# A 4096 x 4096 matrix product with bias and tanh: B's first block in one transfer per column half, visits by column halves, and the last products in another order

## The chip, the cores and the metric

The kernel runs on one core of a Trainium2 chip. The metric is the device time of one execution in microseconds. Below, PE or TensorE is the matrix engine, DVE or VectorE the vector engine, ACT or ScalarE the engine for activations and copies, POOL or GpSimd the engine that here only issues transfers (it casts B and A to fp16 on the way), and SP or SyncE the queue of the other transfers.

## The reference

```python
def reference(a, b, bias):                  # all float32; a, b: 4096 x 4096, bias: 4096
    return np.tanh(np.matmul(a, b) + bias)
```

## The kernel before

The kernel computes in fp16 with float32 sums. B is cut into four column blocks of 1024 columns (`c`), each of two column halves of 512 (`j`). A is cut into 16 pairs of row tiles of 128 rows. K = 4096 stands on the partitions in four quarters of 1024 rows: partition 32q + x holds rows of quarter q. A half of K (`h`) is 16 steps of 128 (`T`), and a step is one matmul of a 128 x 128 piece of A with 128 x 512 of B. Four steps are a block of B (`blk`, `TB`): a tile of 128 partitions x 4 x 512.

Two ways of computing follow each other.

*The opening* treats the first four row pairs, that is eight row tiles m = 0 to 7, of column block 0 with plain products. The eight banks of PSUM hold four row tiles x two column halves. The rows come in visits: first rows 0 to 3 (`g0`) with B's block 0, the sums put aside in SBUF; then rows 4 to 7 (`g1`) with the first half of the first half of K, put aside, while DVE copies rows 0 to 3 back into the banks (`L570`); then rows 0 to 3 again; then rows 4 to 7 again, whose sums DVE brings back with the bias added (`add_bias`, helper line `L85`); then rows 0 to 3 for the last part. Each `mm` (`L424`) has its own weight load. `down` walks along K for one row tile and column half, `across` walks along K over several row tiles and both column halves.

*The rest* uses Strassen's and Winograd's seven products for each pair of rows, pair of column halves and pair of K halves (`items`, `product`, matmuls at `L277`). A's four quadrants (`a11` to `a22`), its differences (`s1` to `s7`, `asum`), B's quadrants (`b11` to `b22`) and its sums (`d1`, `d3`, `d4`, `e6`, `e7`, `bsum`) are the operands. One item takes seven products in the slots of `PRODUCTS` (0: m2, 2: m5, 4: m3, 5: m1, 6: m4, 8: m6, 10: m7), and items overlap: item n + 1 starts seven slots after item n. `after` adds up in PSUM: m2 leaves its sum in bank `z`; DVE reads `z` twice (adds the bias into `d`, puts the temporary `s` into SBUF), and only then may m5 go on adding into `z`.

The order on every engine is written out by hand: `work` maps a slot to what is issued before its products, `second_visit` gives the opening's last part a place in slots -18 to 3, `prepare` and `change` put loads, turns and sums into slots. A slot is one product of 16 matmuls.

What comes first in the program: eight warm-up matmuls on zeros (`fill(WARM, NB)`, helper line `L491`); row tile 0 through SyncE (`coarse`), row tiles 1 to 3 through GpSimd (`first`, `L503`), four transposes on PE for each (`L524`) with more warm-up matmuls between them; B's block 0 of both column halves (`opening_b(("b11", "b12"), 0)`, transfers at `L240`, one for each quarter of K and column half: 32 partitions x 4 x 512); then all further pieces of A for the opening (`land`, `L475`, turned by DVE at `L172`: `g1a`, `g0b`, `g0x`, `g1x`, `g1y`, `g1z`, `g0c`) and of B in the order in which they are used, and the first `nat` tiles (A for the items, `L144`). All of these stand in GpSimd's one queue.

In block 0 of the first half of K the rows of B are laid out so that partition x of a quarter holds rows 4x to 4x + 3; everywhere else it holds rows x, 32 + x, 64 + x, 96 + x of the block.

The column blocks after the first load their B with the same `load_b` (`change`), while the items run.

Of the kernel before, what the change touches and what calls it, by code (L numbers as in the profile page):

```python
# [8 lines left out]
P = 128  # L9
QP = 32  # L10
NB = 512
NCW = 2 * NB
T = 16
TB = 4
TP = T // 2
G = 2
WARM = 8
fp32 = mybir.dt.float32
# [38 lines left out]
def kernel(  # L57
# [167 lines left out]
    def new_bop(name, blk):  # L225
        bop[name, blk] = bops.tile([P, TB, NB], fp16, name=f"{name}_{blk}", tag=f"{name}_{blk}")
        return bop[name, blk]

    def load_b(dst, c, blk, h, j, t0=0, nt=TB):
        dx, dt = (1, QP) if h or blk else (TB, 1)  # L230
        off = b.offset + (h * T * QP + blk * TB * QP + t0 * dt) * N + c * NCW + j * NB
        if nt == 1:
            src = bass.AP(tensor=b.tensor, offset=off, ap=[[KQ * N, 4], [dx * N, QP], [1, NB]])
            nc.gpsimd.dma_start(out=dst[:, t0, :], in_=src)
            return
        for q in (0, 2, 1, 3):
            src = bass.AP(
                tensor=b.tensor, offset=off + q * KQ * N, ap=[[dx * N, QP], [dt * N, nt], [1, NB]]
            )
            nc.gpsimd.dma_start(out=dst[ds(q * QP, QP), ds(t0, nt), :], in_=src)  # L240

    def load_raw(name, c, blk):
        raw[name, blk] = wide.tile([P, TB, NB], fp16, name=name, tag="wide")
# [18 lines left out]


    state, asides = {}, {}

    def product(n, what, left, right):
        c, pairs, part, _ = items[n]
        for s, pair in enumerate(pairs):
            st = state.setdefault((n, s), {})
            where = {"m2": "z", "m5": "z", "m1": "z", "m7": "z", "m3": "c", "m4": "d", "m6": "v"}[what]  # L270
            st[where] = bank(n, s, where)
            ts_ = range(T) if part is None else range(TP)
            for i, t in enumerate(ts_):
                at = aset[n][left][:, t + s * TP, :]
                tb = t if part is None else part * TP + t
                bt = bop[right, tb // TB][:, tb % TB, :]
                nc.tensor.matmul(  # L277
                    st[where], at, bt,
                    start=what == "m2" and i == 0, stop=i == len(ts_) - 1,
                    skip_group_check=True,  # L280
                )
            after(n, s, what, st)
# [6 lines left out]
    def new_out():  # L289
        return outs.tile([P, NB], fp32, name="o", tag="o")  # L290
# [67 lines left out]
    def at_slot(slot, f, *args):  # L358
        work.setdefault(slot, []).append((f, args))

    def prepare(n):

        s0 = SLOTS * (n - 1)
        if again(n):
            at_slot(s0, lambda: aset[n].update((i, aset[n - 2][i]) for i in QUADS))
        elif natural(n):
            at_slot(s0 - 7, load_nat, n, 1)
            at_slot(s0 - 4, load_nat, n, 0)
            turns = (("a22", (0, 0)), ("a21", (2, 2)), ("a11", (3, 4)), ("a12", (5, 5)))
            if n == 0:  # L370
                turns = (("a21", (3, 3)), ("a22", (3, 3)), ("a11", (5, 5)), ("a12", (6, 6)))
            for name, at in turns:
                for u in range(2):
                    at_slot(s0 + at[u], turn, n, name, u)
                at_slot(s0 + at[1], keep, n, name)
        else:
            for name, at in (("a22", 0), ("a21", 1), ("a11", 2), ("a12", 4)):
                at_slot(s0 + at, fetch, n, name)
        late = stays(n)
        at_slot(s0 + 4, asum, n, "s2")  # L380
        at_slot(s0 + 6, asum, n, "s5")
        at_slot(s0 + 9, asum, n, "s1")
        at_slot(s0 + (12 if late else 8 if n else 11), asum, n, "s6")
        at_slot(s0 + (15 if late else 13), asum, n, "s7")

    def change(c, part, n):

# [16 lines left out]

    mb = {}

    def opening_b(names, blk, t0=0, nt=TB):
        for name in names:
            if t0 == 0:
                if name in ("b11", "b22"):  # L410
                    new_bop(name, blk)
                else:
                    raw[name, blk] = wide.tile([P, TB, NB], fp16, name=name, tag="wide")
            dst = bop[name, blk] if name in ("b11", "b22") else raw[name, blk]
            load_b(dst, 0, blk, int(name[1]) - 1, int(name[2]) - 1, t0, nt)

    def right(kt, j):
        h, t = divmod(kt, T)
# [3 lines left out]
    def mm(m, j, kt, start=False, stop=False):  # L422
        h, t = divmod(kt, T)
        nc.tensor.matmul(  # L424
            mb[m % 4, j], aq[m, h][:, t, :], right(kt, j),
            start=start, stop=stop, skip_group_check=True,
        )

    def across(ms, k0, k1, fresh=False):
        for kt in range(k0, k1):  # L430
            for m in ms:
                for j in range(2):
                    mm(m, j, kt, fresh and kt == k0)

    def down(m, j, k0, k1, fresh=False, stop=False):
        for kt in range(k0, k1):
            mm(m, j, kt, fresh and kt == k0, stop and kt == k1 - 1)

    rows4 = [(m, j) for m in range(4) for j in range(2)]
    swapped = [(m, j) for m in (1, 0, 3, 2) for j in range(2)]  # L440
    H1 = (2, 3, 0, 1)
    PLACE = (0, 1, 3, 2)
# [17 lines left out]
    def put_aside(m, j):  # L460
        nc.scalar.copy(spill[m, j], mb[m % 4, j])
# [57 lines left out]
    def turn_first(m, copy):  # L519
        if m == 0:  # L520
            copy(first[:, m], coarse)
        tp = psum.tile([P, TB, P], fp16, name="tp", tag=f"ps_{4 + m}")
        for t in range(TB):
            nc.tensor.transpose(tp[:, t, :], first[:, m, :].rearrange("P q (x t) -> P t (q x)", t=TB)[:, t], ident)  # L524
        for t in range(0, TB, 2):
            copy(aq[m, 0][:, ds(t, 2), :], tp[:, ds(t, 2), :])

    def turn_pair(key):
        for r in range(2):
            turn_in(key, r)  # L530
# [6 lines left out]
    turn_first(2, nc.vector.tensor_copy)  # L537
    fill(2, NB)
    turn_first(3, nc.scalar.copy)
    turn_pair(("g1a", 0))  # L540
    turn_pair(("g1a", 1))
    for j in range(2):
        for m in g0:
            i = 2 * PLACE[m] + j
            mb[m, j] = psum.tile([P, NB], fp32, name=f"ps_{i}", tag=f"ps_{i}")
            down(m, j, 0, TB, True, stop=True)
            put_aside(m, j)
    banks = [mb[PLACE[i // 2], i % 2] for i in range(8)]

    new_spill(1)  # L550
    for p in range(0, 4, 2):
        for j in range(2):
            for m in (p, p + 1):
                down(4 + m, j, 0, TB, True)
    across(g1, TB, TP - 2)
    for m in g0:
        turn_in("g0b", m)
    bias_bc = singles.tile([P, NCW], fp32, name="bias_bc", tag="bias")
# [5 lines left out]
    for blk in H1[:2]:  # L564
        opening_b(("b21", "b22"), blk)
    land(("g1z", 0), 4, T, TP, LAND[0], 2)
    for m, j in rows4:
        down(4 + m, j, TP - 2, TP, stop=True)
        put_aside(4 + m, j)
        nc.vector.tensor_copy(mb[m, j], spill[m, j])  # L570

    for m, j in rows4:
        down(m, j, TB, TP)
    turn_pair(("g0x", 0))
    turn_pair(("g0x", 1))
    land(("g1z", 1), 6, T, TP, LAND[1], 2)
    for blk in H1[2:]:
        opening_b(("b21", "b22"), blk)
    across(g0, TP, T - 2)
    turn_pair(("g1x", 0))  # L580
    turn_pair(("g1x", 1))
    for m, j in rows4:
# [17 lines left out]

    def second_visit(slot):
        if slot < -14:
            for m, j in rows4[2 * (slot + 18):][:2]:
                down(4 + m, j, TP, T)
        elif slot < -8:
            i = slot + 14
            k0 = T + H1[i // 2] * TB + i % 2 * 2
            across(g1, k0, k0 + 2)
        elif slot < -6:
            for m, j in swapped[4 * (slot + 8):][:4]:  # L610
                down(4 + m, j, T + H1[3] * TB, T + (H1[3] + 1) * TB, stop=True)
                end(4 + m, j)
                nc.scalar.copy(mb[m, j], spill[m, j])
        elif slot < 0 or slot in (1, 3):
            m, j = swapped[slot + 6 if slot < 0 else 6 + slot // 2]
            down(m, j, T, 2 * T, stop=True)
            end(m, j)
# [9 lines left out]
    for slot, name, blk in (  # L627
# [4 lines left out]
    ):  # L632
        at_slot(slot, bsum, name, blk)

# [9 lines left out]
    for slot in range(-18, SLOTS * len(items) + 4):  # L644
        for f, args in work.get(slot, ()):
            f(*args)
        second_visit(slot)
        for pos, p in PRODUCTS.items():
            n, r = divmod(slot - pos, SLOTS)
            if r == 0 and 0 <= n < len(items):  # L650
                product(n, *p)


# [28 lines left out]
```

## Time and profile before

| | |
|---|---|
| time, median of 3 runs | 1586.12 us (1585.1 to 1590.45) |
| the profiled execution's own time | 1583.99 us |
| its span | 1582.3 us |
| granted TensorE clock, mean | 0.998 |
| matmuls | 7264 |
| busy: PE, DVE, POOL, ACT | 99%, 58%, 25%, 17% of the span |
| 16 DMA engines, first half of the span by fortieths | 7 to 9 tenths busy |

The span is what the profile covers; 1.7 us of the execution's own time lie around it. "Line" in a row of the profile is the line of the kernel that issued the instruction; `L85` is the helper `tt`, `L172` the helper `transpose`, so these are told apart by their tiles. A row of a timeline is: start, length, engine, line, operation, tiles out<-in, shape, count, and in brackets the idle time of the engine before it with what ended it. A PE row's length holds the modelled end of its last matmul.

### The profile page before, as it was taken

What the parts mean: (1) busy time and instruction counts of PE and PEld (TensorE: products, weight loads), DVE (VectorE), ACT (ScalarE), POOL (GpSimd) and SP (SyncE); (2) the same over time, 40 slices, a digit from 0 to 9 for tenths busy, and PEclk for the clock granted to TensorE, in tenths of its full rate; (3) what the DMA queues carried; (4) which work ended last, traced back from release to release, by engine and by line L of the source; (5) the groups of instructions that cost most, each with busy time, mean ns of one, the idle gap of its engine ahead of it and who ended that gap; (6) DMA issues with size and microseconds to landing.
All of it is one profiled execution on the core that took longest, in us unless ns stands there. A gap on an engine that the chain in (4) does not pass through costs nothing.

```text
span 1582.3 us, 18922 instructions
## 1 busy us (share of the span) xinstructions
PE 1570.2 (99%) x7264; PEld 711.1 (45%) x7264; DVE 917.6 (58%) x1047; ACT 268.2 (17%) x473; POOL 389.0 (25%) x725
## 2 busy tenths in 40 slices
PE   8999999999999999999999999999999999999998
PEld 3444444444444444444444444444444444444443
DVE  3689777777975566577795333333468433333332
ACT  2131111111221111111222111111122111111111
POOL 7764433564441222155440000000140000000000
PEclk9999999999999999999999999999999999999999
DMA  9999977899896776599985444444494444444441
GB/s 167 190 232 223 226 155 166 168 214 224 168 209 190 193 186 161 166 206 231 202 160 165 133 127 140 133 122 143 125 196 118 136 133 133 127 140 134 123 142 48
DMA packets 163674, 259.36 MB, mean 164 GB/s; under 512 B 22784, under 2 KB 84736, under 8 KB 163584
## 3 DMA queue, kind: packets, MB, share of 16 engines
q0 software_dynamic: 94080, 86.42, 37.1%
q1 hardware_dynamic: 69504, 171.74, 32.9%
q8 instruction: 57, 0.93, 0.2%
q14 instruction: 33, 0.27, 0.1%
HBM read 243.27 MB, written 100.66 MB: 217 GB/s over the span
## 4 chain that ended last, share of the span: by engine, by line
PE 98%; DMA 0%; issue 0%; POOL 0%; DVE 0%; ACT 0%; POOLq 0%
PE ps L277 91%; PE ps L424 7%; DMA b<-in_b_dram 0%; POOL first L503 0%; POOL b L240 0%; DVE a L172 0%; DVE o L85 0%; ACT o L350 0%; ACT o L294 0%; DVE s L85 0%; DVE ps L85 0%; POOL ident L505 0%; POOLq L505 0%; POOLq L666 0%
## 5 line engine op out<-in xcount | busy, mean ns | idle before, releaser
L277 PEld LDWEIGHTS <-a 128*128 128x128 f16 x3648 | 357.0, 98 | 430.4
L277 PEld LDWEIGHTS <-s 128*128 128x128 f16 x3072 | 300.6, 98 | 364.2 <-issue 1.9
L277 PE MATMUL ps<-b,s 128*128 128x512 f16 x1920 | 434.0, 379 | 1.6 <-DVE s L85 1.6
L277 PE MATMUL ps<-d,a 128*128 128x512 f16 x1920 | 434.0, 379 | 0.0
L277 PE MATMUL ps<-e,a 128*128 128x512 f16 x1728 | 390.4, 379 | 0.0
L240 POOL DMA_DIRECT2D b<-in_b_dram x256 | 138.5, 549 | 432.9 <-PE ps L277 364.1
L85 DVE TENSOR_TENSOR s<-a,a 128x2048 f16<-128x2048 f16 x192 | 233.0, 1215 | 14.3 <-DMA a<-scratch 13.2
L144 POOL DMA_DIRECT2D nat<-in_a_dram x272 | 143.9, 535 | 309.6 <-DVE a L172 242.8
L277 PE MATMUL ps<-d,s 128*128 128x512 f16 x960 | 217.0, 379 | 0.0
L172 DVE STREAM_TRANSPOSE a<-nat 128x256 f16<-128x256 f16 (+2 forms) x244 | 205.3, 885 | 14.7 <-PE ps L277 9.1
L294 ACT ACTIVATE o<-ps 128x512 f32<-128x512 f32 x180 | 108.1, 601 | 310.6 <-issue 303.8
L85 DVE TENSOR_TENSOR ps<-cs,ps 128x512 f32<-128x512 f32 x60 | 41.4, 695 | 185.9 <-PE ps L277 185.9
L85 DVE TENSOR_TENSOR a<-a,a 128x2048 f16<-128x2048 f16 x108 | 131.4, 1217 | 0.0
L85 DVE TENSOR_TENSOR ps<-ps,s 128x512 f32<-128x512 f32 x72 | 49.3, 696 | 120.7 <-PE ps L277 111.8
L85 DVE TENSOR_TENSOR ps<-ps,bias_bc 128x512 f32<-128x512 f32 x60 | 41.8, 696 | 131.8 <-PE ps L277 131.8
L85 DVE TENSOR_TENSOR o<-ds,ps 128x512 f32<-128x512 f32 x60 | 41.2, 686 | 124.4 <-PE ps L277 86.8
L350 ACT ACTIVATE o<-o 128x512 f32<-128x512 f32 x60 | 37.8, 630 | 372.8 <-DVE o L85 372.8
L335 ACT COPY ds<-ps 128x512 f32<-128x512 f32 x60 | 35.2, 586 | 307.8 <-PE ps L277 307.8
L154 POOL DMA_DIRECT2D nat<-in_a_dram x128 | 68.8, 545 | 43.5 <-DVE a L172 25.7
L424 PE MATMUL ps<-b,oa 128*128 128x512 f16 x256 | 59.0, 393 | 4.9 <-DMA b<-in_b_dram 4.9
L85 DVE TENSOR_TENSOR d<-b,b 128x2048 f16<-128x2048 f16 x48 | 57.2, 1216 | 0.0
L424 PE MATMUL ps<-b,ao 128*128 128x512 f16 x256 | 55.6, 379 | 0.0
(41 smaller groups left out, 406.6 us busy)
## 6 DMA issues: line engine op xcount, KB each, us to landing
out_dram<-o SPq DMA_DIRECT2D x256, 256.0 KB, 3.4
a<-scratch SPq DMA_DIRECT2D x124, 512.0 KB, 4.6
nat<-in_a_dram POOLq DMA_DIRECT2D x272, 128.0 KB, 7.2
b<-in_b_dram POOLq DMA_DIRECT2D x256, 128.0 KB, 5.8
scratch<-a SPq DMA_DIRECT2D x48, 512.0 KB, 6.5
nat<-in_a_dram POOLq DMA_DIRECT2D x128, 64.0 KB, 4.5
scratch<-a SPq DMA_DIRECT2D x32, 256.0 KB, 6.1
land<-in_a_dram POOLq DMA_DIRECT2D x60, 128.0 KB, 5.3
```

Source lines behind the costliest of these rows:

```text
L85: nc.vector.tensor_tensor(out=out_, in0=in0, in1=in1, op=op)
L144: nc.gpsimd.dma_start(out=tl[ds(q * QP, QP), :, :], in_=src.rearrange("(mb p) k -> p mb k", p=QP),)
L154: nc.gpsimd.dma_start(out=tl[ds(q * QP, QP), :, h, :], in_=src.rearrange("(mb p) k -> p mb k", p=QP),)
L172: nc.vector.transpose(dst[:, ds(t, n), :].rearrange("P t (mb p) -> P mb t p", p=QP), src[:, :, ds(t * QP, n * QP)].rearrange(order, x=QP),)
L240: nc.gpsimd.dma_start(out=dst[ds(q * QP, QP), ds(t0, nt), :], in_=src)
L277: nc.tensor.matmul(st[where], at, bt, start=what == "m2" and i == 0, stop=i == len(ts_) - 1, skip_group_check=True,)
L294: nc.scalar.activation(o, src, TANH)
L335: nc.scalar.copy(st["ds"], st["d"])
L350: nc.scalar.activation(o, o, TANH)
L424: nc.tensor.matmul(mb[m % 4, j], aq[m, h][:, t, :], right(kt, j), start=start, stop=stop, skip_group_check=True,)
```

## The change

1. `load_b`: for block 0 of the first half of K (`h == blk == 0`) one transfer covers all 128 partitions, where four covered 32 each. This holds for `b11` and `b12`, in every column block. The arguments for parts of a block go.
2. The plain visits walk by column halves. `across` takes one column half; the first visit of rows 4 to 7 first does all steps, put-asides and copies back of column half 0, then those of column half 1; `byhalf` and `bytwos` are the new orders of (row tile, column half). In `second_visit` two `across` calls of two steps over both halves become calls of four steps, half after half.
3. `fill(8, NB)`: eight more warm-up matmuls on zeros between the last transposes of the opening and the first products.
4. Three sums of B, `d1`, `d4` and `e6` of block 3, go from slots 0, 3 and 5 to slots -5, -4 and -4; `e7` of block 3 goes from slot 7 to slot 5, after `d4` of block 1.
5. In the last item m7 and m6 change places, with their sums `s7` and `s6`. m6, now the last, is done by `last_product`: 16 matmuls of 256 columns for the left half, tanh, store by SyncE; then the same for the right half, with the store issued by ScalarE.

```diff
-    def load_b(dst, c, blk, h, j, t0=0, nt=TB):
-        dx, dt = (1, QP) if h or blk else (TB, 1)
-        off = b.offset + (h * T * QP + blk * TB * QP + t0 * dt) * N + c * NCW + j * NB
...
+    def load_b(dst, c, blk, h, j):
+        off = b.offset + (h * T + blk * TB) * QP * N + c * NCW + j * NB
+        if h == blk == 0:
+            src = bass.AP(tensor=b.tensor, offset=off, ap=[[KQ * N, 4], [N, QP * TB], [1, NB]])
+            nc.gpsimd.dma_start(out=dst, in_=src)
             return
         for q in (0, 2, 1, 3):
             src = bass.AP(
-                tensor=b.tensor, offset=off + q * KQ * N, ap=[[dx * N, QP], [dt * N, nt], [1, NB]]
+                tensor=b.tensor, offset=off + q * KQ * N, ap=[[N, QP], [QP * N, TB], [1, NB]]
             )
...
+    def last_product(n, left, right):
+
+        c, (pair,), part, _ = items[n]
+        st = state[n, 0]
+        for half in (ds(0, NB // 2), ds(NB // 2, NB // 2)):
+            for t in range(T):
+                nc.tensor.matmul(
+                    st["v"][:, half], aset[n][left][:, t, :],
+                    bop[right, t // TB][:, t % TB, half],
+                    start=False, stop=t == T - 1, skip_group_check=True,
+                )
+            o = new_out()
+            nc.scalar.activation(o[:, half], st["v"][:, half], TANH)
+            queue = nc.sync if half.start == 0 else nc.scalar
+            queue.dma_start(
+                out=out[ds((2 * pair + 1) * P, P), ds(c * NCW + NB + half.start, NB // 2)],
+                in_=o[:, half],
+            )
...
-        at_slot(s0 + (12 if late else 8 if n else 11), asum, n, "s6")
-        at_slot(s0 + (15 if late else 13), asum, n, "s7")
+        end_ = n == len(items) - 1
+        at_slot(s0 + (12 if late else 13 if end_ else 8 if n else 11), asum, n, "s6")
+        at_slot(s0 + (15 if late else 12 if end_ else 13), asum, n, "s7")
...
-    def across(ms, k0, k1, fresh=False):
+    def across(ms, j, k0, k1):
         for kt in range(k0, k1):
             for m in ms:
-                for j in range(2):
-                    mm(m, j, kt, fresh and kt == k0)
+                mm(m, j, kt)
...
+    byhalf = [(m, j) for j in range(2) for m in range(4)]
+    bytwos = [(m + r, j) for m in (0, 2) for j in range(2) for r in range(2)]
...
     turn_first(3, nc.scalar.copy)
+    fill(8, NB)
...
-    across(g1, TB, TP - 2)
...
-    for m, j in rows4:
+    for m, j in byhalf:
+        if m == 0:
+            across(g1, j, TB, TP - 2)
         down(4 + m, j, TP - 2, TP, stop=True)
         put_aside(4 + m, j)
         nc.vector.tensor_copy(mb[m, j], spill[m, j])
 
-    for m, j in rows4:
+    for m, j in byhalf:
         down(m, j, TB, TP)
...
-    across(g0, TP, T - 2)
+    for k0, k1 in ((TP, TP + TB), (TP + TB, T - 2)):
+        for j in range(2):
+            across(g0, j, k0, k1)
...
-        (-6, "e6", 0), (-5, "d3", 3), (0, "d3", 1), (0, "d1", 3), (1, "d1", 1),
-        (3, "d4", 3), (4, "d4", 1), (5, "e6", 3), (6, "e6", 1), (7, "e7", 3),
+        (-6, "e6", 0), (-5, "d3", 3), (-5, "d1", 3), (-4, "d4", 3), (-4, "e6", 3),
+        (0, "d3", 1), (1, "d1", 1), (4, "d4", 1), (5, "e7", 3), (6, "e6", 1),
...
-                product(n, *p)
+                if n < len(items) - 1 or p[0] not in ("m6", "m7"):
+                    product(n, *p)
+                elif p[0] == "m6":
+                    product(n, *PRODUCTS[10])
+                else:
+                    last_product(n, *PRODUCTS[8][1:])
```

More of the change, by code (lines that the diff above doesn't have):

```diff
@@ L227, in new_bop @@
         return bop[name, blk]
-    def load_b(dst, c, blk, h, j, t0=0, nt=TB):
-        dx, dt = (1, QP) if h or blk else (TB, 1)
-        off = b.offset + (h * T * QP + blk * TB * QP + t0 * dt) * N + c * NCW + j * NB
-        if nt == 1:
-            src = bass.AP(tensor=b.tensor, offset=off, ap=[[KQ * N, 4], [dx * N, QP], [1, NB]])
-            nc.gpsimd.dma_start(out=dst[:, t0, :], in_=src)
+    def load_b(dst, c, blk, h, j):
[3 more added lines that the diff above has]
+            nc.gpsimd.dma_start(out=dst, in_=src)
             return
@@ L237, in load_b @@
             src = bass.AP(
-                tensor=b.tensor, offset=off + q * KQ * N, ap=[[dx * N, QP], [dt * N, nt], [1, NB]]
+                tensor=b.tensor, offset=off + q * KQ * N, ap=[[N, QP], [QP * N, TB], [1, NB]]
             )
-            nc.gpsimd.dma_start(out=dst[ds(q * QP, QP), ds(t0, nt), :], in_=src)
+            nc.gpsimd.dma_start(out=dst[ds(q * QP, QP)], in_=src)
     def load_raw(name, c, blk):
@@ L405, with opening_b @@
     mb = {}
-    def opening_b(names, blk, t0=0, nt=TB):
+    def opening_b(names, blk):
         for name in names:
[L409 to L415, printed above, removed]
+            if name in ("b11", "b22"):
+                load_op(name, 0, blk)
+            else:
+                load_raw(name, 0, blk)
     def right(kt, j):
@@ L539 @@
     turn_first(3, nc.scalar.copy)
+    fill(8, NB)
     turn_pair(("g1a", 0))
     turn_pair(("g1a", 1))
[L542 to L547, printed above, removed]
+    for m, j in byhalf:
+        i = 2 * PLACE[m] + j
+        mb[m, j] = psum.tile([P, NB], fp32, name=f"ps_{i}", tag=f"ps_{i}")
+        down(m, j, 0, TB, True, stop=True)
+        put_aside(m, j)
     banks = [mb[PLACE[i // 2], i % 2] for i in range(8)]
     new_spill(1)
[L551 to L554, printed above, removed]
-    across(g1, TB, TP - 2)
+    for m, j in bytwos:
+        down(4 + m, j, 0, TB, True)
     for m in g0:
@@ L570 @@
         nc.vector.tensor_copy(mb[m, j], spill[m, j])
-    for m, j in rows4:
+    for m, j in byhalf:
         down(m, j, TB, TP)
@@ L602, in second_visit @@
         if slot < -14:
-            for m, j in rows4[2 * (slot + 18):][:2]:
+            for m, j in bytwos[2 * (slot + 18):][:2]:
                 down(4 + m, j, TP, T)
         elif slot < -8:
-            i = slot + 14
-            k0 = T + H1[i // 2] * TB + i % 2 * 2
-            across(g1, k0, k0 + 2)
+            i, j = divmod(slot + 14, 2)
+            across(g1, j, T + H1[i] * TB, T + (H1[i] + 1) * TB)
         elif slot < -6:
@@ L650 @@
             if r == 0 and 0 <= n < len(items):
-                product(n, *p)
+                if n < len(items) - 1 or p[0] not in ("m6", "m7"):
+                    product(n, *p)
+                elif p[0] == "m6":
+                    product(n, *PRODUCTS[10])
+                else:
+                    last_product(n, *PRODUCTS[8][1:])
 _INS = ['a', 'b', 'bias']
```

## The prediction, made before the changed kernel had run

> **What bounds the kernel now.** First the page, for the engine that carries the time, then the waits of that engine.
>
> ```profile
> PE 1570.2 (99%) x7264; PEld 711.1 (45%) x7264; DVE 917.6 (58%) x1047; ACT 268.2 (17%) x473; POOL 389.0 (25%) x725
> ```
> ```profile
> PE ps L424 <- DMA b<-in_b_dram: 4.9, 1, 4.9
> PE ps L277 <- DVE s L85: 1.6, 1, 1.6
> ```
> TensorE is busy for 99% of the span and waits in two places: 4.9 us for B's first block, 1.6 us for VectorE. Warm matmuls of 512 columns start 0.216 us apart. The change removes no product, so it can win only at the start, at that one wait and at the end. The chain of waits, in order of time (start, length, what), shows the three places:
>
> ```profile
> 5.68 6.36 DMA b<-in_b_dram
> 12.17 106.64 PE ps L424 x480
> 124.88 1.20 DVE a L172
> 126.67 0.59 DVE s L85
> 127.30 3.61 PE ps L277 x16
> 1577.95 0.70 DVE o L85
> 1578.67 0.63 ACT o L350
> ```
> The chain hides what nearly ended later. For that, the timelines of GpSimd (its transfer issues) and VectorE, and the windows (PEclk is the fourth column from the end, after POOL):
>
> ```profile
> 4.06 4.31 POOL L240 DMA_DIRECT2D b<-in_b_dram  x8
> 9.47 0.59 POOL L475 DMA_DIRECT2D land<-in_a_dram  x1 [1.10 <-DMA b<-in_b_dram]
> ...
> 14.71 1.23 POOL L475 DMA_DIRECT2D land<-in_a_dram  x2 [0.29 <-DMA b<-in_b_dram]
> 16.04 3.26 POOL L240 DMA_DIRECT2D b<-in_b_dram  x5
> ```
> ```profile
> 11.50:14.90 3.40, 2.73 (x7) 1.05 (x8) 0.00 (x0) 0.59 (x1) 2.50 (x5) 0.50 1.26 174
> 14.90:18.30 3.40, 3.40 (x10) 1.17 (x9) 0.39 (x1) 1.17 (x2) 2.84 (x6) 0.54 1.43 190
> ```
> ```profile
> 53.00 2.37 DVE L172 STREAM_TRANSPOSE ao<-land 128x1024 f16<-128x1024 f16 x2 [0.34 <-DMA land<-in_a_dram]
> 55.30 4.87 DVE L85 TENSOR_TENSOR ps<-spill,bias_bc 128x512 f32<-128x512 f32 x8
> ...
> 107.81 3.56 DVE L172 STREAM_TRANSPOSE a<-nat 128x256 f16<-128x256 f16 x4 [2.67 <-DMA nat<-in_a_dram]
> ...
> 116.70 3.56 DVE L172 STREAM_TRANSPOSE a<-nat 128x256 f16<-128x256 f16 x4 [0.67 <-DMA nat<-in_a_dram]
> ...
> 121.44 2.35 DVE L85 TENSOR_TENSOR d<-b,b 128x2048 f16<-128x2048 f16 x2
> ```
> GpSimd keeps eight transfers open and issues the next when the oldest has landed. From 16.04 to 19.45 five issues go out, each released by a landing: 0.68 us a transfer of 128 KB. This one queue runs almost without a pause until item 0's last `nat` transfer lands at 116.6. VectorE waits for it at 53.00, 107.81 and 116.70. So TensorE, though nearly always busy, has little slack to this queue: the second visit of rows 4 to 7 starts at 56.50, and the bias add that it needs (first of the eight at 55.30, 0.6 us each) ends at 55.95, 0.55 us sooner.
>
> **The change part by part**, against the profiled execution: 1583.99 us, 1.7 more than its span, and 2.1 below the median of the runs, 1586.12.
>
> *B's first block.* Eight issues of 0.545 us (4.31 us) become two. A transfer of 512 rows into 128 partitions is L503's: 0.78 us, so 1.6. That is off the path, since the transfers, not the issues, are slow. After `first` (last landing 6.63) the eight quarters land at 9.18, 10.22, 11.39, 12.04, 12.73, 13.56, 14.43 and 15.08: 8.45 us, where 8 x 0.68 = 5.4 would do. So the queue can come forward by 3.0 at most (Y) and by nothing at least. The loss lies in the first quarters, 2.5, 1.0 and 1.2 us each. If they stall one after another because each is the first touch of its own part of B, one transfer that touches all four parts at once pays the longest stall (2.55 - 0.68 = 1.9) and saves the rest of the 3.0, 1.1; if they stall because one quarter alone fills 32 partitions, all 3.0 go. I take Y = 2.3, in the upper half, since the `first` transfers over 128 partitions land 3.3 us after their issue and show no such loss. The first matmul then starts near 10.1, not 12.17. Later column blocks get the same transfer; there L240's transfers have ended no wait of TensorE.
>
> *Longer warm-up.* Eight more matmuls start at 7.3 and take 8 x 0.216 = 1.7, to 9.0: idle time is used, nothing is delayed unless B lands before 9.0. Now the idle 4.87 us bring the clock to half from 11.5 to 18.3 (the two windows): 14.4 matmuls' worth, 3.1 us. Filled, the gap is about 1 us and I expect full clock.
>
> *What becomes of both.* TensorE alone would be 2.1 + 3.1 = 5.2 sooner, at the second visit by 51.3. But the bias add stands behind the transposes of the `land` tile at 53.00, and is sooner only by Y: 55.95 - 2.3 = 53.65. So TensorE waits there 2.3, and 2.85 of the 5.2 are left. Without the warm-up it would arrive 0.75 after the add, and the next place takes that back. So the clock, 3.1 us by itself, is worth nothing at Y = 2.3.
>
> *Three B sums sooner.* d1, d4 and e6 of block 3 (1.14 us apart, 3.4 in all) move to VectorE's place after 101.6, where it idles 2.23 and 2.67 for `nat`: hidden, 4.9 against 3.4. If the idle were gone, only the 0.67 before 116.70 would be left to absorb them: 2.8 later. The 1.6 wait: item 0's s5, the two sums at 121.44, the a12 transposes and two adds that free the bank stand in one unbroken run from 116.70 to 127.25. One of the two sums leaves it: -1.14. The run starts with the last `nat` landing, so it also moves by Y: m5 starts at 127.30 - 1.14 - 2.3 = 123.86. TensorE arrives at 125.56 - 2.85 = 122.7 and waits 1.2. So the opening gains 1.14 + Y = 3.4, whatever TensorE itself gained.
>
> *Visits by column halves*: as many matmuls, each with its own weight load as before (7264 and 7264); the second half of a block is wanted later. I take 0: no wait stands there, b11's second block lands by 23.1 and is wanted at 28.9. If 5.2 us were gone and Y nothing, 0.6 would still cover it.
>
> *Last products.* m6 ends the kernel in two halves of 256 columns. L524's matmuls of 128 columns start 56 ns apart, those of 512 216, so 256 take 109 and 32 of them 3.49, not 3.45. The second half adds a wait: its first matmul writes the bank that the first TANH reads, and waits for it. Last issue 1.64, result 1.91, TANH at 2.00; 0.39 long (a 256-column copy 0.375, a 512-column TANH 0.601); matmuls again at 2.44, where 1.75 was possible; last result 4.35 after the product's start, now 3.61. Behind it stood 0.09 + 0.69 + 0.03 + 0.63 = 1.44 of subtraction and TANH, now 0.09 + 0.39. Net 1.44 - 0.48 - 0.74 = 0.2; the store is half as large, ScalarE issues it, and no row shows a ScalarE issue: the last store now lands 2.0 after issue, `coarse` from SyncE took 3.1. Between -0.7 and +0.6 in all; I take 0.3, near SyncE's row.
>
> Sum: 3.4 + 0.3 = 3.7. Profiled 1580.3, median 1582.4, 0.23% faster. A measurement of this kernel can tell 0.3%, 4.8 us, from no change.
>
> **The rivals.**
>
> *Every saving counts* (2.1 + 3.1 + 1.7 + 0.3 = 7.2: 1578.9), or Y is full at 3.0 (4.4: 1581.7). For: the waits of TensorE name only B and VectorE. Against the first: the 0.55 us at 55.95, where `land` gates whatever TensorE does.
>
> *B's first rows are slow however fetched.* Y = 0: 1.14 + 0.3, 1584.7. For: the second half's quarters, same rows, took 0.65 to 0.87. Against: first quarters of later blocks run at 0.68.
>
> *Four engines, not sixteen* (the slower side). The new transfer's source is an outer loop over 4 quarters of B, its target one over 128 partitions; if it is dealt out by the 4, each of four engines moves 128 rows. A 128-row quarter over sixteen takes 0.68, so 8 rows take 0.68 and 128 take 10.9. From 6.3, b11 lands at 17.3, 5.2 later than now. The clock falls as now; m5 is ready at 125.56 + 5.2, 3.5 later than today's 127.30: with the tail 3.2 slower, 1589.3. If both halves share the same four, b12 lands at 28 and TensorE waits 4 more: 1593. It decides from a first matmul later than about 14.2. For: no transfer of the trace has so short an outer loop on one side. Against: every one whose target is 128 partitions lands like its neighbours. The Trainium skill (DMA: Bandwidth & Descriptors, "Why a DMA increments its semaphore by 16 and not by 1") says that a transfer runs on the largest number of engines up to 16 that divides the slowest dimension on both sides, which would be 4 here, and names an exception in which GpSimd's direct copies are dealt by partitions; by the rule the sum is this rival's, by the exception mine, and no run here shows which.
>
> *Sums in the way*: `nat` lands early and the three sums delay the transposes: up to 2.8 lost of 3.7, 1585.2.
>
> **How the numbers follow.** My forecast 50% (own range 1581.4 to 1584.3; about a quarter of it may measure beyond 0.3%: 13 faster, 37 same). All or full Y 20%, faster. Slow B 8%, same. Four engines 17%: half beyond the bound. Other losses 5%, slower. Faster 33, same 53, slower 14. The range 1578.8 to 1589.5 takes in the first rival's 1578.9 and four engines' 1589.3, and leaves out the shared four and what is unforeseen.
>
> **What would show it.** Right: two L240 issues of 0.8 at 4.06; first L424 matmul at 9.5 to 10.7, in the gap eight warm matmuls; PEclk 1.0 from 11.5; b12 landed near 12.8; a new wait of PE ps for VectorE near 52, about 2 us, another near 123, about 1; at the end a wait for ScalarE of 0.7. Wrong: a first matmul after 14 (four engines), no wait near 52 (every saving counts), VectorE without idle time before the a21 transposes (sums in the way).

## The result, and the profile after

The changed kernel takes 1603.24 us (median of 5 runs, 1602.85 to 1604.33) against 1587.1 us for the kernel before (5 runs on the same chip): a ratio of 1.0103, 95% interval 1.0088 to 1.0118. It is 1% slower, where the forecast was 0.23% faster, and lies 14 us above the upper end of the range. The profiled execution has a span of 1601.0 us; the one of before had 1582.3.

First the page's engine row and the waits of TensorE (waited for: us in total, times, longest):

```profile
PE 1575.9 (98%) x7288; PEld 713.7 (45%) x7288; DVE 918.3 (57%) x1047; ACT 268.3 (17%) x474; POOL 383.2 (24%) x701
```
```profile
PE ps L295 <- DVE ps L85: 10.2, 2, 5.2
PE ps L440 <- DMA b<-in_b_dram: 9.6, 1, 9.6
...
PE ps L271 <- ACT o L277: 0.5, 1, 0.5
```
The wait for B's first block has doubled, 4.9 to 9.6. The wait of m5 for `s`, 1.6 us before, is gone. A new pair of waits has come, 10.2 us together, which no step of the prediction had. The chain of waits tells where they stand:

```profile
4.06 15.35 DMA b<-in_b_dram
19.55 105.59 PE ps L440 x480
...
379.09 20.06 DMA b<-in_b_dram
399.44 4.92 DMA b<-in_b_dram
404.49 1.23 DVE d L85
...
409.78 305.34 PE ps L295 x1408
...
772.09 20.56 DMA b<-in_b_dram
792.93 4.91 DMA b<-in_b_dram
...
803.21 790.04 PE ps L295 x3648
```
Three of the eight single transfers stand in these rows: `b11` of the opening, 15.35 us from issue to landing, and one of about 20 us at each of two column changes, where column block 0 gives way to 1 (near 400 us) and 1 to 2 (near 797). Behind each of the latter two stands one more transfer, 4.9 us, then a sum of B on VectorE. GpSimd's timeline shows why a transfer that is not wanted at once stops what is behind it:

```profile
379.09 1.56 POOL L233 DMA_DIRECT2D b<-in_b_dram  x1 [2.95 <-issue]
380.65 3.79 POOL L239 DMA_DIRECT2D b<-in_b_dram  x7
399.44 0.55 POOL L239 DMA_DIRECT2D b<-in_b_dram  x1 [15.00 <-DMA b<-in_b_dram]
```
GpSimd issues the single transfer (1.56 us) and seven quarters. Then eight are open, the oldest is the single one, and the queue stands for 15.0 us until that lands at 399.16; the quarters issued at 380.65 land only behind it, from 399.8 on. At 399.44 the quarter that `d` waits for goes out. What TensorE makes of it:

```profile
409.78 4.89 PE L295 MATMUL ps<-d,a 128*128 128x512 f16 x16 [4.92 <-DVE ps L85]
```
```profile
803.21 6.13 PE L295 MATMUL ps<-d,a 128*128 128x512 f16 x16 [5.23 <-DVE ps L85]
```
It idles 4.92 and 5.23 us, the granted clock falls to 0.50 (from 410 to 412, and from 803 to 808), and the next sixteen matmuls take 4.89 and 6.13 where sixteen at full clock take 3.62. At the third change, near 1190, no wait stands. The last single transfer before it went out at 1157.57, 34.9 us before the product that stands in the same place (1192.50); at the first two it went out 25.8 and 25.9 us before that product was due. So there is 9 us more room at the third, and 21.6 us from issue to landing still fit.

The sum, from these rows: m5 of item 0 starts at 131.88, before at 127.30: +4.6. Idle time at the two changes 4.92 + 5.23 = +10.15. Slow clock behind them 1.27 + 2.51 = +3.8. From the start of the last product to the end of the span 7.95 by the trace, before 8.01: -0.06. Together 18.5 of the 18.7 us between the spans.

### The profile page after: what moved, and what is told of

It is laid out like the page before. It is cut to its first block, busy times and chain, and to the rows that moved or that the text cites. A ratio compares the mean times of both kernels' runs of the same rounds, so it can differ in the third digit from the quotient of the medians.

```text
span 1601.0 us, 18943 instructions
## 1 busy us (share of the span) xinstructions
PE 1575.9 (98%) x7288; PEld 713.7 (45%) x7288; DVE 918.3 (57%) x1047; ACT 268.3 (17%) x474; POOL 383.2 (24%) x701
## 2 busy tenths in 40 slices
DMA packets 175722, 259.41 MB, mean 162 GB/s; under 512 B 34704, under 2 KB 96912, under 8 KB 175632
## 4 chain that ended last, share of the span: by engine, by line
PE 88%; DMA 8%; DVE 1%; POOL 1%; issue 1%; ACT 0%; DVEq 0%; POOLq 0%; ACTq 0%
PE ps L295 80%; PE ps L440 7%; DMA b<-in_b_dram 7%; DMA nat<-in_a_dram 2%; POOL nat L154 1%; DVE s L85 0%; DVE a L172 0%; DVE d L85 0%; PE ps L271 0%; POOL b L233 0%; DVE ps L85 0%; POOL first L520 0%; DVE a L85 0%; POOL b L239 0%; ACT o L277 0%
## 5 line engine op out<-in xcount | busy, mean ns | idle before, releaser
L295 PE MATMUL ps<-d,a 128*128 128x512 f16 x1920 | 437.8, 382 | 10.2 <-DVE ps L85 10.2
L239 POOL DMA_DIRECT2D b<-in_b_dram x224 | 121.2, 546 | 132.3 <-DMA b<-in_b_dram 77.5
L233 POOL DMA_DIRECT2D b<-in_b_dram x8 | 12.5, 1569 | 321.3 <-PE ps L295 300.3
```

The lines of the kernel that those rows point to most:

```text
L233: nc.gpsimd.dma_start(out=dst, in_=src)
L239: nc.gpsimd.dma_start(out=dst[ds(q * QP, QP)], in_=src)
L295: nc.tensor.matmul(st[where], at, bt, start=what == "m2" and i == 0, stop=i == len(ts_) - 1, skip_group_check=True,)
```

## The experiments

**Theory 1**: the whole loss is the single transfer, at three places: the opening and two column changes. Its source is an outer loop over four quarters, so it is dealt to four DMA engines. **Theory 2**: the other parts (visits by halves, warm-up, last products) cost as well; or the transfer is slow because of its size (512 rows) or its 128 partitions. The kernels were measured in three groups on three chips, each beside the kernel before, whose medians there are 1585.71 us (16 runs, for the single transfer and all quarters), 1585.98 (19, for the outer loops) and 1586.47 (25, for warm-up and sums). Each ratio is to the kernel before of its own group.

**All quarters, the rest of the change kept.**

```diff
-        if h == blk == 0:
+        if False:
...
+        dx, dt = (1, QP) if h or blk else (TB, 1)
```


> B's first blocks come in four quarters each again; visit order, longer warm-up, earlier sums and swapped last products stay. Theory 1 (all of the loss is the single transfer): first matmul near 12.2 again, no wait of TensorE for B at the two column changes (now 4.9 and 5.2 us), and what is left of the change is the sum that leaves the run before m5, 1.1, and the end, 0.2 to 0.4: about 1.4 under the kernel before, ratio near 0.999. Theory 2 (visit order, warm-up or last products cost as well): slower than the kernel before by over 3 us.

Measured: 1585.78 us, ratio 1.0002, interval 0.9985 to 1.0020. The 17.5 us between the changed kernel and this one are the single transfer's. So the other parts cost less than 3.2 us together, which excludes the first half of theory 2 beyond that. A gain of 1.4 lies inside the interval and is not shown. The runs spread from 1582.4 to 1593.0, and the profiled one was the slowest (1592.98), which makes it worth reading. TensorE's timeline and then the chain of waits ahead of m5:

```profile
12.00 8.59 PE L441 MATMUL ps<-b,oa 128*128 128x512 f16 x32 [2.73 <-DMA b<-in_b_dram]
...
58.12 41.60 PE L441 MATMUL ps<-b,ao 128*128 128x512 f16 x192 [1.94 <-DVE ps L85]
...
134.09 5.53 PE L296 MATMUL ps<-b,s 128*128 128x512 f16 x16 [5.61 <-DVE s L85]
```
```profile
124.78 4.60 DMA nat<-in_a_dram
129.38 1.20 DVE d L85
130.59 2.28 DVE a L172 x2
132.87 0.59 DVE ps L85
133.46 0.59 DVE s L85
134.09 5.53 PE ps L296 x16
```
These are the two places of the prediction: the bias add at the second visit, and m5 behind VectorE's unbroken run, which follows the landing of `nat`. In this execution TensorE arrives ahead of VectorE at both, and waits.

**The single transfer alone, on the kernel before.**

```diff
+        if h == blk == 0:
+            src = bass.AP(tensor=b.tensor, offset=off, ap=[[KQ * N, 4], [N, QP * TB], [1, NB]])
+            nc.gpsimd.dma_start(out=dst, in_=src)
+            return
```


> The kernel before with the single transfer alone. Theory 1: the whole loss and no gain, about 1.4 us more than the changed kernel's 1603.2, so 1604 to 1605, ratio 1.011; first matmul at 19.5, waits for B at both column changes. Theory 2: clearly below 1603, by what the other parts cost.

Measured: 1604.13 us, ratio 1.0119 (1.0102 to 1.0137). First matmul at 19.82, waits of 12.2 us for B and 9.7 at two column changes: the whole loss, as theory 1 has it. The profiled execution, the slowest of the four (1606.13), has one more wait, 3.0 us for VectorE's `s` at 160.5, which the changed kernel does not have.

**The single transfer in column block 0 alone, and at the later blocks alone.**

```diff
-        if h == blk == 0:
+        if h == blk == c == 0:          # the first kernel
+        if h == blk == 0 and c > 0:     # the second kernel
```


> The changed kernel with the single transfer in the first column block alone, quarters at the later ones. Theory 1, by the places: the opening as in the changed kernel (first matmul 19.5, m5 at 131.9, so 4.6 over before), no wait near 402 and 797; the two changes give back about 7 us each: 1589 to 1591, 3 to 5 over the kernel before. If the loss all came from a late opening, it stays near 1603.

> The changed kernel with quarters in the first column block and the single transfer at the later ones. Theory 1: opening as in the kernel before less 1.1 (m5 near 126), then two waits of TensorE for B and the sums behind it at the first two column changes, about 7 us each with the clock's fall: 1598 to 1600. If later transfers are hidden, as my prediction had it, 1585.

Measured: 1589.84 us, ratio 1.0028 (1.0017 to 1.0039), and 1597.48 us, ratio 1.0077 (1.0057 to 1.0096). The waits of TensorE in the first, then in the second:

```profile
PE ps L441 <- DMA b<-in_b_dram: 11.4, 1, 11.4
PE warm L509 <- DVE zeros L503: 1.3, 1, 1.3
PE ps L272 <- ACT o L278: 0.5, 1, 0.5
```
```profile
PE ps L296 <- DVE ps L85: 9.9, 2, 5.1
PE ps L441 <- DMA b<-in_b_dram: 2.7, 1, 2.7
```
The first has the opening's wait and none at the changes; the second has the two waits at the changes (9.9 us), and its m5 starts at 126.46, where 126 was expected. Over the median of all quarters the opening costs 4.1 and the changes 11.7. The second kernel came out 0.5 under the lower end of what was expected. The two parts add up to 15.8 of the 17.5; the interval of the second is 3 us wide to each side, so the rest is not resolved.

**What makes it slow: the outer loop.** The same transfer, with 16, 8 and 2 pieces in the outer loop of its source instead of 4. These kernels leave out rows of B that the product needs and take others in their place:

```diff
-            src = bass.AP(tensor=b.tensor, offset=off, ap=[[KQ * N, 4], [N, QP * TB], [1, NB]])
+            src = bass.AP(tensor=b.tensor, offset=off, ap=[[64 * N, 16], [N, 32], [1, NB]])    # 16
+            src = bass.AP(tensor=b.tensor, offset=off, ap=[[128 * N, 8], [N, 64], [1, NB]])    # 8
+            src = bass.AP(tensor=b.tensor, offset=off, ap=[[512 * N, 2], [N, 256], [1, NB]])   # 2
```


> The changed kernel, but the outer loop of the single transfer's source runs over 16 pieces of 32 rows instead of 4 quarters of 128 (these are other rows of B, so the output leaves the right rows of the first blocks out; bytes, row length, partitions and number of transfers are the same). Theory 1 (the transfer is dealt to as many engines as its outer loop counts, 4): on sixteen engines the first block lands 5 to 7 us after its issue (15.4 now), first matmul near 10 to 11, no wait of TensorE at the column changes; the time falls to that of the kernel before or under it, 1582 to 1586. Theory 2 (size: 512 rows in one transfer, or 128 partitions, is slow by itself): landing stays at 15, time at 1603.

> The same with an outer loop of 8 pieces of 64 rows (other rows of B again). Theory 1: eight engines, half the rows for each: landing of the first block 8 to 10 us after issue, so a first matmul at 12.5 to 14, and 9 to 11 us for the transfers at the column changes: 1585 to 1590. Theory 2: 1603.

> The same with an outer loop of 2 pieces of 256 rows (other rows of B again). Theory 1: two engines, twice the rows for each: landing of the first block 27 to 31 us after issue, first matmul at 31 to 35, single transfers at the column changes 30 to 40 us, and a time of 1625 to 1650. Theory 2: 1603.

The DMA issues of the kernels with an outer loop of 16, 8, 4 (the changed kernel) and 2, in this order; the last column is the median from issue to landing:

```profile
b<-in_b_dram POOLq DMA_DIRECT2D x8, 512.0 KB, 7.8
```
```profile
b<-in_b_dram POOLq DMA_DIRECT2D x8, 512.0 KB, 10.4
```
```profile
b<-in_b_dram POOLq DMA_DIRECT2D x8, 512.0 KB, 19.0
```
```profile
b<-in_b_dram POOLq DMA_DIRECT2D x8, 512.0 KB, 29.6
```
Same bytes, same rows of 512 numbers, same 128 partitions, same number of transfers. The first of each run, `b11`, meets the emptiest queue: 7.57, 10.13, 15.35 and 26.02 us. The steps are 2.56, 5.22 and 10.67, each about twice the last. With 512/k rows on each of k engines that is 5.0 + 0.083 x 512/k: 7.7, 10.3, 15.6 and 26.3. So k is the outer loop, and size and partitions are not the reason.

The number of engines shows more directly late in a single transfer, when share and rate stand still. A window ends with the clock, the DMA share (mean of the 16 engines; overlapping packets bring it to 1.2 to 1.4 where all are at work) and GB/s. This one is the changed kernel's, with `b11` and `b12` both open:

```profile
16.00:18.00 2.00, 0.00 (x0) 0.00 (x0) 0.00 (x0) 0.00 (x0) 0.00 (x0) 0.50 0.62 104
```
Two transfers of 4 pieces show a share of 0.62 and 104 GB/s. One of them alone (397.5 to 399.0) shows 0.31 and 51, and one of 2 pieces alone (424 to 428 of that kernel) 0.15 and 26. Share and rate double with the pieces, and they double with a second transfer, so the two halves of B stood on different engines. Four engines of sixteen at 1.24 would be 0.31.

The times: 1583.36 us (ratio 0.9991, 0.9973 to 1.0009) at 16, 1584.01 (0.9981, 0.9964 to 0.9997) at 8, and one run of 1668.13 at 2. Neither of the first two has a wait at a column change. The last was expected at 1625 to 1650 and missed that, since at 2 all three changes wait (59.4 us in three waits), where at 4 two do. The others missed in part as well: at 16 and 8 the first block landed 0.6 and 0.1 us later than the ranges given, the first matmul came at 11.74 and 14.35 (10 to 11 and 12.5 to 14 were expected), and at 8 the time is 1 us under its range. At 2 the first block landed 1 us sooner than expected.

The kernel with 8 says most about the opening. Its TensorE timeline:

```profile
14.35 9.79 PE L440 MATMUL ps<-b,oa 128*128 128x512 f16 x32 [4.41 <-DMA b<-in_b_dram]
...
127.57 3.62 PE L295 MATMUL ps<-b,s 128*128 128x512 f16 x16
```
The first product comes 2.2 us later than in the kernel before, at half clock as there, and yet the time is 0.03 to 0.36% lower: from 14.35 on TensorE does not wait until the last product.

**Without the longer warm-up, and with far too much of it** (on the kernel with all quarters).

```diff
-    fill(8, NB)                     # the first kernel
+    fill(44, NB)                    # the second kernel, instead of fill(8, NB)
```


> Quarters, without the eight matmuls more of warm-up; visit order, sums and last products as changed. If TensorE's early arrival is worth nothing because VectorE and the transfer queue set the second visit (near 56) and m5 (near 126): the first 32 matmuls take 10.0 again instead of 8.5, the waits behind them shrink by that, and the median stays within 1.5 us of the kernel with quarters and the longer warm-up (1585.8). If the clock counted, 1.4 to 3.1 slower.

> Quarters, with 44 matmuls of extra warm-up instead of 8: TensorE is kept at full clock and the first product is held back on purpose to about 17, so that the second visit starts near 58, behind what the queue delivers. If a late start behind the queue costs only its own lateness and takes the queue's chance delays with it, no wait of TensorE stands between the first product and the last: about 1582.5 to 1584.5 with a spread under 2 us (with quarters and 8 matmuls 1582.4 to 1593.0). If an early start is worth its time, 4 to 5 us slower than with quarters: 1590.

Measured: 1583.9 us (ratio 0.9983, 0.9967 to 0.9998) without, 1585.34 (0.9991, 0.9979 to 1.0003) with 44, against 1585.78 with 8. TensorE's timelines, without and with 44:

```profile
10.99 3.61 PE L441 MATMUL ps<-b,oa 128*128 128x512 f16 x16 [2.64 <-DMA b<-in_b_dram]
...
129.03 5.30 PE L296 MATMUL ps<-b,s 128*128 128x512 f16 x16 [2.90 <-DVE s L85]
```
```profile
17.10 7.07 PE L441 MATMUL ps<-b,oa 128*128 128x512 f16 x32
...
130.11 5.30 PE L296 MATMUL ps<-b,s 128*128 128x512 f16 x16 [2.34 <-DVE s L85]
```
A first product at 10.99, 12.00 or 17.10 makes no difference that these runs can tell. Both profiled executions, each the slowest of its ten, come to m5 ahead of VectorE. Both expectations missed in part. Without the warm-up the 32 matmuls were to be slow again, but after the 2.64 us of idle in this execution the clock had not fallen (1.00 from 11 to 20), and a second wait for B, 1.47 us, stands between the first sixteen and the next; so this trace does not show what a low clock would cost. With 44 the wait at the second visit went, as expected, but in the profiled execution (1588.78) m5's stayed, 2.34 us. The nine other runs lie within 1.1 us, 1584.47 to 1585.58, which is the narrow spread that was expected, at 0.8 us above the range for the median; whether m5 waited in them no trace shows.

The version without the longer warm-up is the best of those that compute the whole product: 0.17% under the kernel before, and 1.2% under the changed kernel. Its interval is just clear of 1, but it is one of several that were tried, so the 0.17% are weak evidence.

**The three B sums back at their old slots** (on the kernel with all quarters).

```diff
-        (-6, "e6", 0), (-5, "d3", 3), (-5, "d1", 3), (-4, "d4", 3), (-4, "e6", 3),
-        (0, "d3", 1), (1, "d1", 1), (4, "d4", 1), (5, "e7", 3), (6, "e6", 1),
+        (-6, "e6", 0), (-5, "d3", 3), (0, "d3", 1), (0, "d1", 3), (1, "d1", 1),
+        (3, "d4", 3), (4, "d4", 1), (5, "e6", 3), (6, "e6", 1), (7, "e7", 3),
```


> Quarters, with the three B sums of block 3 at their old places. If they stand in the unbroken run of VectorE before m5, as the prediction had it, m5's wait is about 1.1 longer and the median 1.1 over the kernel with quarters, about the kernel before plus 0 to 1. If that run is not what ends the wait, no difference.

Measured: 1587.24 us, ratio 0.9998 (0.9980 to 1.0016); all quarters had 1.0002. The medians differ by 1.5 in the expected direction, the ratios by nothing. With runs spread over 8 to 11 us an effect of 1.1 can't be seen here: inconclusive.

## Why the prediction was wrong

**The step that failed is the first term, B's first block.** The prediction weighed sixteen engines against four and took sixteen, with Y = 2.3. The transfer ran on four. `b12` was forecast at 12.8 and landed at 21.43: in the prediction's terms Y = -6.35. It gave as evidence against four that every transfer with a target of 128 partitions lands like its neighbours; in those rows the outer loop of the source was 128 as well, so they could not tell the two apart. The trace had no row with a short outer loop, as the prediction itself says. The Trainium skill (DMA: Bandwidth & Descriptors, "Why a DMA increments its semaphore by 16 and not by 1") has a transfer run on the largest number of engines up to 16 that divides the slowest dimension of both sides, which would be 4 here, and 16, 8 and 2 in the experiments. The landings and the DMA shares agree. The exception that it names for some of GpSimd's direct copies, dealing by partitions, did not apply to this copy: 15.35 us where the outer loop of 16 took 7.57.

**The rival had the mechanism at 17% and the wrong size.** Its price per row was right: 10.9 us for 128 rows, measured 0.083 x 128 = 10.7. Its fixed part was too small: it let the rows run from 6.3, while the landings put the start at 4.06 + 5.0 = 9.1; so a landing at 17.3 became 19.41, and +3.2 became +4.1 to +4.6. Its turning point, "a first matmul later than about 14.2", agrees with the kernel of outer loop 8, which started at 14.35 and lost nothing. The fear that both halves share the same four engines did not come true: `b12` landed 2.0 behind `b11`, not 10.

**The largest loss had no price at all.** "Later column blocks get the same transfer; there L240's transfers have ended no wait of TensorE." That was true of quarters that land in 5.8 us. It costed six further transfers at nothing without saying how late they could be. The answer lies between 10.4 and 19.0 us: at 10.4 no change waits, at 19.0 two of three do. From the waits it can be estimated closer: at the first two changes the transfer landed 20.06 and 20.56 us after its issue and TensorE waited 4.92 and 5.23, so a landing within about 15.2 us would have cost nothing there. The later blocks make 11.7 (by the medians) to 13.9 us (by the profile) of the whole loss, and without them the rival's time, 1589.3, would have been 0.5 from the 1589.84 measured.

**Issue cost.** Two of 0.78 were forecast from `first`; with four engines they took 1.57 each, with sixteen 0.74. That was not on the path.

**Y on sixteen engines.** With an outer loop of 16, `b12` landed at 14.63, before at 15.08: Y = 0.45, near the rival "slow however fetched" (Y = 0) and not the 2.3 chosen. That pair is two executions: in the profiled kernels with quarters in column block 0, the one before among them, the last of `b12` lands anywhere from 14.85 to 16.68, so Y lies between 0.2 and 2.1, below 2.3 in each. The median of that kernel, 1583.36, is 1.0 from the 1582.4 forecast, and its interval holds both that and no change.

**The clock and TensorE's early arrival** were judged rightly as far as the runs can tell: worth nothing, because the bias add at the second visit and then m5 behind the `nat` landings hold TensorE. With quarters the new wait near 56 is there (1.94, 1.4 without the warm-up), and the first product could move by 6 us without an effect. What the prediction did not see is how much the wait of m5 changes: none to 5.6 us in the profiled executions of the twelve kernels. That it comes from the queue's timing, and that it makes the spread of one kernel's runs, fits but is not shown, since each kernel has one trace.

**The sums**: with quarters and the single transfer at the later blocks m5 started at 126.46; the prediction's sum at Y = 0 gives 127.30 - 1.14 = 126.16. The other kernels with quarters in block 0 and the sums moved had it at 129.03 to 134.09, so this one agreement may be chance. In time the gain is not shown. **The end**: the stall between the halves was to be 0.69 and is 0.52, TANH 0.39 and is 0.38; from the start of the last product to the end of the span 8.01 became 7.94 to 7.96, a gain of 0.05 to 0.07, where 0.3 was taken from -0.7 to +0.6. **Visits by halves** showed no loss, but were not run by themselves.

## What to carry to other kernels

Before several transfers are joined into one, look at the outermost loop of both sides of its access pattern: here the number of engines that it got followed from that loop, and four times the bytes on a quarter of the engines is a late transfer that also holds up the queue behind it. A change in a shared helper has to be priced at every place that calls it, with the lateness from which each place would start to wait. And before time at the start is counted as a gain, find the next place where another engine's queue holds TensorE: here the first product could come 6 us sooner or later for nothing.

## What the runs showed of the hardware

- A GpSimd transfer with a short outer loop, and so few engines, also has more small packets. Packets under 512 B on the page: 22416, 26512, 34704 and 51088 with an outer loop of 16, 8, 4 and 2. For each of the eight transfers that is 512 x (16/k - 1) more than at 16, and the issue takes 0.74, 1.03, 1.57 and 2.56 us.
- The clock's fall does not follow from the length of the gap alone. After 1.86 us (outer loop 16) and 2.64 us (without the longer warm-up) of idle time before the first product the 216 ns pace went on; after 2.73 us (all quarters) the clock was 0.50 from 12.0 to 14.8, and after 4.41 us (outer loop 8) likewise. Ahead of m5 shorter gaps were enough: after 2.34 us (44 warm-up matmuls) and 2.50 us (outer loop 16) the clock was 0.50 from 132 to 134 and from 130 to 132. The windows of the kernel with outer loop 8 show the fall and the return (granted clock third from the end):

```profile
10.00:12.00 2.00, 0.00 (x0) 0.00 (x0) 0.00 (x0) 0.00 (x0) 0.00 (x0) 1.00 1.19 180
...
14.00:16.00 2.00, 1.65 (x4) 0.59 (x5) 0.00 (x0) 0.00 (x0) 0.58 (x1) 0.50 1.52 181
...
20.00:22.00 2.00, 2.00 (x11) 0.88 (x9) 1.69 (x4) 1.26 (x3) 1.61 (x4) 1.00 1.14 172
```
The Trainium skill (TensorE: Matmul & The Clock Gate, Part 1: The HAM clock gate) describes a window of about 3.4 us that runs freely and is not reset when a kernel starts. The traces agree: the half-clock stretches inside the kernels last 3.41, 6.83, 10.24 us and further multiples of 3.41, and a gap of 2.34 us fell where one of 2.64 did not.
- Some kernels had hardly any spread: 0.7 us over 7 runs (single transfer in block 0 alone), 1.3 over 8 (outer loop 8) and 1.5 over 5 (the changed kernel), against 6 to 11 for those with quarters in block 0 and a warm-up of none or 8 over ten runs. In the traces of the first three m5 does not wait for VectorE, and their first products come at 14.35 or later. The kernel with 44 warm-up matmuls starts at 17.10, and nine of its ten runs lie within 1.1 us, which fits a late start as the reason; the tenth, with the wait, lies 3.2 above them. Why VectorE was late there although TensorE started late is left open.
